# Residual adds and sums of squares of two token quarters moved from VectorE to GpSimd, with the residual's steps two ticks apart, in a hybrid decoder layer

## The chip, the cores and the metric

The kernel is one program on one core of a Trainium2 chip. The metric is the device time of one execution in microseconds, as the median of several runs. Engine names in the profile: PE is TensorE (PEld its weight loads), DVE is VectorE, ACT is ScalarE, POOL is GpSimd, SP is SyncE, which here issues all DMAs of the stage in question.

## The reference, cut to what matters

One decoder layer over 2048 tokens of width 1024, all in f32. Two groups of token mixers (gated DeltaNet and HGRN2, four heads each) give `mix`. Then, with `rms_norm(x, w) = x * rsqrt(mean(x * x) + eps) * w` over the width:

```python
mix_out = jnp.einsum('btc,cd->btd', mix, w_out[i])
h = h + rms_norm(mix_out, post_mix_norm[i])
u = jnp.einsum('btd,df->btf', rms_norm(h, pre_mlp_norm[i]), w_mlp_up[i])
y = jnp.einsum('btf,fd->btd', jnp.square(jax.nn.relu(u)), w_mlp_down[i])
h = h + rms_norm(y, post_mlp_norm[i])
e = rms_norm(jnp.einsum('bte,ed->btd', p[i], w_ple_proj[i]), ple_norm[i])
gate = jax.nn.sigmoid(jnp.einsum('btd,de->bte', h, w_ple_gate[i]))
h = h + e * gate
```

The change lies in the first three of these lines: the output projection, the residual with its norm, and the norm ahead of the up projection.

## The kernel before, in words

**Layout.** The width stands on the 128 partitions, so a matrix of 1024 by 512 tokens is eight tiles of 128x512. The tokens are four quarters `q` of 512. Every f32 matmul operand is split in two fp32r halves, a high one (a ScalarE copy, line 159 or 212) and a low one (a VectorE subtraction, line 160 or 213), and each product of two such operands is three matmuls.

**The output projection** (lines 1283 to 1327) runs over 32 tiles `j`, that is `(q, d)`: four quarters times eight output tiles of 128 columns. A tile is 24 matmuls (`product`, line 1092). `ready_out(j + 2)` and `stage_out(j + 3)` prepare weights ahead: for the first three quarters the raw weights `raw_out` are loaded and split (1024 columns wide, one ScalarE and one VectorE instruction); for the last quarter both halves are reloaded from a copy in DRAM, without a split. After each tile ScalarE copies the PSUM bank to `yo` (line 1319) and squares it; `squares` (line 215) adds the square to `acc_o`. The squares use one buffer, tag `sq`, `bufs=1`, which the norms also use.

**Ticks.** `mm` (line 1085) calls `tick()` ahead of every eighth matmul. `later(gen, offsets)` enters a generator in an agenda; each tick runs one step of what is due. An output tile is three ticks. This sets the order in which instructions are written down; each engine then runs its own queue in that order as a scheduler arranged it, with TensorE's order fixed by hand.

**Norm and residual of the first two quarters.** When a quarter's eight tiles are done, `normed` (line 1169) is entered with the offsets `OUT_STEPS`:

- the first two steps are `rstd_steps` (line 1115): split `acc` to `hl`; then a ones-matmul of two (lines 1121 and 1122) sums over partitions, and ScalarE (Ln, Exp, Square) with VectorE (lines 1125 to 1131) makes `r`, the reciprocal root;
- eight steps of `residual` (line 1148): store the tile before to `h1d`, load the next tile of `x` (tag `late`, two buffers), then `y = y * gain * r` (line 1159), `y = y + x` (line 1160), and through `squares` the square of `y` summed into `acc_h` (line 223);
- one step stores the last tile and splits `acc_h`, and one step is again the norm, which gives `rn`, kept in `h1_r[q]`.

The third and fourth quarters only store `yo` and the norm's row; their residual comes later, inside the up projection (`passed`, line 1180).

**Preparing the up projection.** The up projection is a Strassen product with seven combinations of weight blocks and of columns. `early_operands` (line 1211), entered at tile (2, 1), reloads the first quarter from `h1d`, scales it by `rn` (line 1218) and splits it. Once `h1_r[1]` is there, `up_operands` (line 1222), called `prep`, does the same for the second quarter (line 1237), forms differences (lines 1241, 1242, 1247, 1252) and splits them, one step a tick. The weight blocks come from `u_raw`: blocks "11" and "12" are split at the last tile but one, "22" at the last, with the sums of lines 1303 and 1304; blocks "1", "2" and "4" follow after the last tile (lines 1328 to 1332). The first group of the up projection then multiplies "11" and "12", and after that the other five blocks together, column by column.

**Order on the queues.** SP issues in its own order and waits in place: a store to `h1d` waits for the residual add of its tile, and later loads stand behind it.

Of the kernel before, what the change touches and what calls it, by code (L numbers as in the profile page):

```python
# [15 lines left out]
ALU = mybir.AluOpType  # L16
# [7 lines left out]
KD = D // P  # L24
QT = 512
NQ = T // QT
# [11 lines left out]
R_PREMIX, R_POSTMIX, R_PREMLP, R_POSTMLP, R_PLE = 0, 8, 16, 24, 32  # L38
# [5 lines left out]
N_CONST = C_MASK + len(LEVELS)  # L44


OUT_STEPS = (1, 5) + tuple(range(7, 15)) + (15, 25)
MLP_STEPS = (1, 5) + tuple(range(7, 25, 2))


# [33 lines left out]
def trunk(ctx, tc, x, xT, pT, vecs, w_in, w_ab, gdn_a_log, gdn_dt_bias, w_out, w_up, w_down,  # L84
          w_ple, w_gate, consts, out):
    nc = tc.nc
    V, S, G, PE = nc.vector, nc.scalar, nc.gpsimd, nc.tensor
# [13 lines left out]
    def bank(name, pool=None):  # L101
        return (pool or pm).tile([P, QT], F32, tag="ps", name=name)

    def blk(c):
        return slice(c * P, (c + 1) * P)
# [14 lines left out]
    def col(r):  # L120
        return cols[:, r : r + 1]
# [35 lines left out]
    def split(t, eng, raw):  # L157

        S.activation(t[:, 0], raw, AF.Copy)  # L159
        eng.tensor_tensor(t[:, 1], raw, t[:, 0], ALU.subtract)  # L160
# [54 lines left out]
    def squares(acc, src, k, name, eng=V):  # L215

        if acc is None:
            acc = st.tile([P, QT], F32, tag="acc", name=f"acc_{name}", bufs=3)
            S.activation(acc, src, AF.Square)
        else:  # L220
            sq = st.tile([P, QT], F32, tag="sq", name=f"sq_{name}_{k}", bufs=1)
            S.activation(sq, src, AF.Square)  # L222
            eng.tensor_tensor(acc, acc, sq, ALU.add)  # L223
        return acc
# [7 lines left out]
    def spread_load(rd, name, pool=None, tag="rsb", bufs=2):  # L232
        rsb = (pool or st).tile([P, QT], F32, tag=tag, name=f"rsb_{name}", bufs=bufs)
        nc.sync.dma_start(rsb, rd.broadcast_to([P, QT]))
        return rsb
# [8 lines left out]
    def tok(q):  # L244
        return slice(q * QT, (q + 1) * QT)

    mixd = [[dr.tile([P, QT], F32, name=f"mixd{q}_{k}") for k in range(KD)] for q in range(NQ)]
    h1d = [[dr.tile([P, QT], F32, name=f"h1d{q}_{k}") for k in range(KD)] for q in range(NQ)]
# [99 lines left out]
    with ExitStack() as ectx:  # L348
        es = ectx.enter_context(tc.tile_pool(name="es", bufs=1))
        with tc.manual_schedule(engines={mybir.EngineType.SP}):  # L350
# [34 lines left out]
            rsb = spread_load(x_r[0], "x0")  # L385
# [10 lines left out]
    with mixers as mctx:  # L396
# [605 lines left out]
        with tc.manual_schedule(engines={mybir.EngineType.SP}):  # L1002
# [5 lines left out]
            for j, (name, key, src, q, h, then, g, b) in enumerate(works):  # L1008
# [3 lines left out]
                ps = bank(f"mm_{name}")  # L1012
# [40 lines left out]
            while clock[0] <= last or len(held) < 2 or 1 in ready:  # L1053
                if fill:
                    q, d = fill.pop(0)
# [25 lines left out]
    def later(gen, offsets):  # L1081
        for o in offsets:
            agenda.setdefault(clock[0] + o, []).append(gen)
# [24 lines left out]
    def late(src, name):  # L1108
        t = st.tile([P, QT], F32, tag="late", name=name)
        nc.sync.dma_start(t, src)  # L1110
        return t
# [3 lines left out]
    def rstd_steps(acc, scale, eps, name, done, pool=None, home=None, wait=False):  # L1115

        hl = st.tile([P, 2, QT], F32R, tag="hl", name=f"hl_{name}", bufs=1)
        split(hl, V, acc)
        yield
        ps = bank(f"nrm_{name}", pool or pp)  # L1120
        PE.matmul(ps, ones, hl[:, 0, :], start=True, stop=False)
        PE.matmul(ps, ones, hl[:, 1, :], start=False, stop=True)
        r = home() if home else st.tile([P, QT], F32, tag="rsb", name=f"r_{name}", bufs=2)
        t = st.tile([P, QT], F32, tag="sq", name=f"rr_{name}", bufs=1)
        V.tensor_scalar(acc, ps, scale, eps, ALU.mult, ALU.add)
        S.activation(r, acc, AF.Ln)
        S.activation(r, r, AF.Exp, scale=-0.5)
        S.activation(t, r, AF.Square)
        V.tensor_tensor(t, t, acc, ALU.mult)
        V.tensor_scalar(t, t, -0.5, 1.5, ALU.mult, ALU.add)  # L1130
        V.tensor_tensor(r, r, t, ALU.mult)
        if wait:
            yield
        done(r)
# [10 lines left out]

    kept_rows = []

    def residual(q, y_of, rsb, skip, gain, dst, name, sums=None):

        xk = late(skip(0), f"x{name}{q}_0")  # L1150
        y = y_of(0)
        total, put = None, None
        for d in range(KD):
            yield
            if put:
                nc.sync.dma_start(*put)
            if d + 1 < KD:
                nxt, ynxt = late(skip(d + 1), f"x{name}{q}_{d + 1}"), y_of(d + 1)
            V.scalar_tensor_tensor(y, y, col(gain + d), rsb, ALU.mult, ALU.mult)
            V.tensor_tensor(y, y, xk, ALU.add)  # L1160
            put = dst[d], y
            if sums is not None:
                total = squares(total, y, d, f"{sums}{q}")
            xk, y = nxt, ynxt
        yield
        nc.sync.dma_start(*put)
        return total

    def normed(q, ys, acc, skip, gain, dst, name, sums=None, pool=None):

        rd = []
        yield from rstd_steps(acc, 1.0 / D, EPS, f"{name}{q}", rd.append, pool)
        total = yield from residual(q, lambda d: ys[d], rd[0], skip, gain, dst, name, sums)
        if sums is not None:
            yield from rstd_steps(total, 1.0 / D, EPS, f"{sums}{q}", partial(h1_r.__setitem__, q), pool,
                                  lambda: tp.tile([P, QT], F32, tag="rsn", name=f"rn{q}"))
# [17 lines left out]
    def run(gen):  # L1194
        for _ in gen:
            pass
# [73 lines left out]
    def u_block(n, t, raw):  # L1270
        x[n] = t
        split(t.rearrange("p h k n -> p h (k n)"), V, raw)

    def two_blocks(*them):

        w = wp.tile([P, 2, KD, P], F32R, tag="whl", name=f"w_u{them[0][0]}")
        halves = [w[:, :, : KD // 2], w[:, :, KD // 2 :]]
        for t, it in zip(halves, them):
            if it:
                u_block(it[0], t, it[1])  # L1280
        return halves[1]

    for j, (q, d) in enumerate(order):
        if d == 0:
            ys, acc = [], None
            if q < 2:
                later(mix_operands(q + 1), range(2, 18, 2))
            if q == 1:
                later(mix_operands(3), range(17, 25))
        ready_out(j + 2)  # L1290
        stage_out(j + 3)
        if j == len(order) - 5:
            u_raw = [wp.tile([P, 2, QT], F32, tag="raw", name=f"u_raw{i}", bufs=2) for i in range(2)]
            a1, a2 = w_up[0], w_up[FF // P // 2]
            for t, i, src in ((u_raw[0], 0, a1[:, : KD // 2]), (u_raw[1], 1, a1[:, KD // 2 :]),
                              (u_raw[0], 1, a2[:, : KD // 2]), (u_raw[1], 0, a2[:, KD // 2 :])):
                nc.sync.dma_start(t[:, i].rearrange("p (k n) -> p k n", n=P), src)
        if j == len(order) - 2:
            two_blocks(("11", u_raw[0][:, 0]), ("12", u_raw[1][:, 1]))
        if j == len(order) - 1:  # L1300
            (a11, a21), (s1, s4) = ((t[:, 0], t[:, 1]) for t in u_raw)
            b22 = two_blocks(("22", s1), None)
            V.tensor_tensor(s1, s1, a21, ALU.add)
            V.tensor_tensor(a21, a11, a21, ALU.subtract)
            u_block("3", b22, a21)
        if (q, d) == (2, 1):
            early = early_operands()
            later(early, range(KD))
        if prep is None and h1_r[1] is not None:
            run(early)  # L1310
            prep = up_operands(0, h1_r)
            later(prep, range(0, 24, 1))
        if j in held:
            ps = held.pop(j)
        else:
            ps = bank(f"mmo_{q}_{d}", pp)
            product(ps, columns(ready.pop(j)), xin[q])
        y = ytile(f"yo{q}_{d}") if q < 2 else tp.tile([P, QT], F32, tag="stg", name=f"yo{q}_{d}")
        S.activation(y, ps, AF.Copy)
        acc = squares(acc, ps, d, f"o{q}")  # L1320
        ys.append(y)
        if q >= 2:
            nc.sync.dma_start(yod[q][d], y)
        if d == KD - 1 and q < 2:
            later(normed(q, ys, acc, lambda d, q=q: xT[blk(d), tok(q)], R_POSTMIX, h1d[q], "o", "h"), OUT_STEPS)
        elif d == KD - 1:
            later(rstd_steps(acc, 1.0 / D, EPS, f"o{q}", row_of(o_r, q), po, wait=True), OUT_STEPS[:2] + (9,))
    b2 = two_blocks(("1", s1), None)
    V.tensor_tensor(a11, s1, a11, ALU.subtract)
    u_block("2", b2, a11)  # L1330
    V.tensor_tensor(s4, s4, a11, ALU.subtract)
    u_block("4", wp.tile([P, 2, KD // 2, P], F32R, tag="raw", name="w_u4", bufs=2), s4)
    run(prep)
    octx.close()
# [323 lines left out]
    rsb = {q: spread_load(ple_r[q], f"pg{q}", None, "acc", 3) for q in (0, 1)}  # L1658
    es, puts = {(q, 0): embedded(q, 0, rsb[q]) for q in (0, 1)}, []
    for half in range(2):  # L1660
# [4 lines left out]
        for d in range(KD):  # L1665
# [4 lines left out]
            if d + 1 == KD and half == 0:  # L1670
                rsb = {q: spread_load(ple_r[q], f"pg{q}", None, "acc", 3) for q in (2, 3)}
            for s, q in enumerate(qs):
                ps = bank(f"mmg_{q}_{d}", pp)
# [60 lines left out]
```

## Time and profile before

| what | us |
|---|---|
| median of 3 runs | 2756.56 |
| lowest and highest run | 2754.08, 2765.73 |
| the profiled execution | 2763.47 |
| its span (first to last instruction) | 2761.6 |
| output projection in that trace, first to last matmul | 1136 to 1330 |
| up projection in that trace, first matmul | 1330 |

All times inside the trace are counted from the start of the span. A profile line of an instruction has its start, its duration, the engine, the line of the kernel, the operation, output and inputs by name, shapes and count; in brackets stands the idle time of the engine ahead of it and what ended it. A merged line (x24) has the time from the first start to the last end. Recorded durations of successive instructions on VectorE and ScalarE overlap a little, so what one instruction occupies is read from the next one's start. In a line of waits the numbers are the total in us, how often, and the longest. In a line of one tile's instructions the numbers in the middle are the shortest, median and longest duration in ns, then the first and last start. In the table of stretches PEclk, the granted TensorE clock, is the third number from the end, followed by the DMA share and GB/s.

### The profile page before, as it was taken

The page shows a single profiled execution, that of the slowest core. Times are in us where ns is not written, and L with a number is a line of the kernel's source. Part 1 is how long each engine was busy: PE and PEld are TensorE (multiplying, and loading weights), DVE is VectorE, ACT ScalarE, POOL GpSimd, SP SyncE. Part 2 cuts the span into 40 slices and gives each one's busy share as a digit, 9 for nine tenths or more (in the row PEclk, how much of TensorE's full clock was granted, in tenths as well). Part 3 has the DMA queues.
Part 4 walks back from the last instruction along what each step waited for, and adds up shares of the span by engine and source line. Part 5 has one row for each costly group of instructions (what it writes and reads, how often), then busy time and mean ns, then how long its engine had stood idle before and what let it go on. Part 6 is the DMA issues. An engine that isn't in the chain of part 4 may idle for free.

```text
span 2761.6 us, 38372 instructions
## 1 busy us (share of the span) xinstructions
PE 2672.5 (97%) x12721; PEld 2219.0 (80%) x12721; DVE 2045.6 (74%) x4242; ACT 1469.3 (53%) x2943; POOL 104.4 (4%) x104
## 2 busy tenths in 40 slices
PE   7999999999999999999899999999999999999999
PEld 5788788888888888777788887887888888887887
DVE  6788777787777777577889867857787765567776
ACT  6665555464546445676555645545454545465421
POOL 0000000000000000000000000001000000001000
PEclk9999999999999999999999999999999999999999
DMA  7776776666666665787466547667464456677663
GB/s 262 250 250 224 231 250 234 224 220 226 234 210 217 200 213 174 262 303 246 146 221 221 187 164 245 220 193 241 152 207 147 146 177 203 193 254 236 209 207 133
DMA packets 268598, 589.24 MB, mean 213 GB/s; under 512 B 55642, under 2 KB 59960, under 8 KB 249200
## 3 DMA queue, kind: packets, MB, share of 16 engines
q1 hardware_dynamic: 268400, 586.79, 63.7%
q8 instruction: 101, 1.65, 0.3%
q14 instruction: 97, 0.79, 0.1%
HBM read 419.75 MB, written 166.92 MB: 212 GB/s over the span
## 4 chain that ended last, share of the span: by engine, by line
PE 57%; DVE 9%; DMA 6%; issue 5%; ACT 3%; POOL 1%; SPq 1%; DVEq 0%; POOLq 0%; ACTq 0%
PE u L1090 21%; PE d L1090 20%; PE mmg L1090 6%; PE mm L1020 6%; DVE pr_g L658 1%; DMA ud_g<-u_g 1%; DMA sys_g<-ud_g 1%; PE mmo L1090 1%; DVE xs_g L661 1%; DMA rd_g<-m_g 1%; DMA rsb_g<-rd_g 1%; DMA raw_out<-in_w_out_dram 1%; DVE xs_g L663 1%; DMA db<-hid 1%; DMA mixT<-mixd 0%
## 5 line engine op out<-in xcount | busy, mean ns | idle before, releaser
L1020 PE MATMUL mm<-xt,w 128*128 128x512 f32 x3072 | 771.2, 399 | 3.1 <-ACT qk_h L758 1.5
L1020 PEld LDWEIGHTS mm<-xt,w 128*128 128x128 f32 x3072 | 560.4, 189 | 109.8 <-ACT qk_h L758 1.9
L1090 PE MATMUL d<-db,da 128*128 128x512 f32 x2688 | 617.2, 391 | 6.9 <-ACT db L212 4.9
L1090 PEld LDWEIGHTS d<-db,da 128*128 128x128 f32 x2688 | 507.0, 189 | 116.3 <-ACT db L212 6.7
L1090 PE MATMUL u<-t,wu 128*128 128x512 f32 x2604 | 593.3, 390 | 3.5 <-ACT wu L159 3.4
L1090 PEld LDWEIGHTS u<-t,wu 128*128 128x128 f32 x2604 | 489.6, 188 | 106.4 <-ACT wu L159 4.2
L213 DVE TENSOR_TENSOR db<-db 128x512 fp32r<-128x512 f32 x224 | 160.8, 718 | 76.0 <-ACT db L212 74.8
L1419 DVE TENSOR_TENSOR u<-u,u 128x512 f32<-128x512 f32 x224 | 150.5, 683 | 63.1 <-PE u L1090 61.1
L212 ACT ACTIVATE db<-db 128x512 fp32r<-128x512 f32 x224 | 140.9, 629 | 85.2 <-DMA db<-hid 81.2
L1090 PE MATMUL mmo<-mixT,w_out 128*128 128x512 f32 x720 | 169.2, 395 | 9.6 <-DVE w_out L160 7.1
L1090 PE MATMUL mmg<-h2T,wg 128*128 128x512 f32 x768 | 174.5, 389 | 0.0
L1460 ACT ACTIVATE u<-u 128x512 f32<-128x512 f32 x128 | 80.9, 632 | 168.0 <-DVE u L1419 167.7
L1090 PEld LDWEIGHTS mmo<-mixT,w_out 128*128 128x128 f32 x720 | 137.0, 191 | 40.9 <-DVE w_out L160 8.8
L1090 PEld LDWEIGHTS mmg<-h2T,wg 128*128 128x128 f32 x768 | 144.2, 188 | 29.9
L160 DVE TENSOR_TENSOR da<-da 128x512 fp32r<-128x512 f32 x128 | 94.2, 736 | 88.3 <-ACT da L159 87.9
L159 ACT ACTIVATE da<-da 128x512 fp32r<-128x512 f32 x128 | 80.5, 629 | 136.9 <-DMA da<-sumd 114.7
L159 ACT ACTIVATE wu<-a 128x512 fp32r<-128x512 f32 x124 | 73.9, 622 | 49.2 <-DMA a<-in_w_up_dram 46.6
L658 DVE TENSOR_TENSOR pr_g<-xs_g,sys_g 128x16 f32<-128x16 f32 (+14 forms) x240 | 93.9, 391 | 5.3
L223 POOL TENSOR_TENSOR acc_y<-acc_y,sq_y 128x512 f32<-128x512 f32 x28 | 38.6, 1380 | 1384.1 <-ACT sq_y L222 1383.3
L160 DVE TENSOR_TENSOR wu<-a,wu 128x512 fp32r<-128x512 f32 x124 | 84.9, 688 | 3.9 <-ACT wu L159 3.8
L1461 ACT ACTIVATE u<-u 128x512 f32<-128x512 f32 x128 | 80.7, 631 | 3.7
L160 DVE TENSOR_TENSOR da<-dr,da 128x512 fp32r<-128x512 f32 x96 | 66.3, 691 | 18.2 <-ACT da L159 16.3
(374 smaller groups left out, 3806.9 us busy)
## 6 DMA issues: line engine op xcount, KB each, us to landing
w<-cache_in SPq DMA_DIRECT2D x96, 1024.0 KB
db<-hid SPq DMA_DIRECT2D x224, 256.0 KB
cache_in<-w SPq DMA_DIRECT2D x32, 1024.0 KB
hid<-u SPq DMA_DIRECT2D x128, 256.0 KB
da<-sumd SPq DMA_DIRECT2D x128, 256.0 KB
a<-in_w_up_dram SPq DMA_DIRECT2D x124, 256.0 KB
hid<-ht SPq DMA_DIRECT2D x96, 256.0 KB
dr<-in_w_down_dram SPq DMA_DIRECT2D x96, 256.0 KB
```

The lines of the kernel that those rows point to most:

```text
L159: S.activation(t[:, 0], raw, AF.Copy)
L160: eng.tensor_tensor(t[:, 1], raw, t[:, 0], ALU.subtract)
L212: S.activation(t[:, 0], plain(t), AF.Copy)
L213: V.tensor_tensor(t[:, 1], plain(t), t[:, 0], ALU.subtract)
L223: eng.tensor_tensor(acc, acc, sq, ALU.add)
L658: V.tensor_tensor(pr[:, :, :, 0:i], xs[:, None, :, 0:i].broadcast_to([P, 2, GC, i]), sys[:, 0:i, i : i + 2].rearrange("p j two -> p two j" ...
L661: V.tensor_reduce(xs[:, :, i : i + 2].rearrange("p g two -> p two g"), pr[:, :, :, 0 : i + 1], AX.X, ALU.add)
L1020: PE.matmul(ps, *terms[i], start=i == 0, stop=i == nt - 1)
L1090: PE.matmul(ps, a, b, start=start, stop=stop)
L1419: V.tensor_tensor(c[new], c[old], ps, ALU.add)
L1460: S.activation(c[k], c[k], AF.Relu)
L1461: S.activation(c[k], c[k], AF.Square)
```

## The change

The residual of the first two quarters gets an engine argument: its adds run on GpSimd, and so do its sums of squares but for the last one of each quarter, which stays on VectorE. The sums of squares of the fourth quarter's projection go to GpSimd as well. The offsets in ticks become 3 and 6 for the norm (1 and 5 before), 9, 11, ... 23 for the eight residual tiles (7 to 14 before), 24 and 27 for the last store and second norm (15 and 25 before). The third and fourth quarters' norms, which use the first two offsets, move with them from 1, 5, 9 to 3, 6, 9. `early_operands` takes every second tick from the third on, where it took every tick. Two subtractions of weight blocks are written down ahead of the last tile and no longer behind it.

```diff
-OUT_STEPS = (1, 5) + tuple(range(7, 15)) + (15, 25)
+OUT_STEPS = (3, 6) + tuple(range(9, 25, 2)) + (24, 27)
...
-    def residual(q, y_of, rsb, skip, gain, dst, name, sums=None):
+    def residual(q, y_of, rsb, skip, gain, dst, name, sums=None, eng=V):
...
-            V.tensor_tensor(y, y, xk, ALU.add)
+            eng.tensor_tensor(y, y, xk, ALU.add)
             put = dst[d], y
             if sums is not None:
-                total = squares(total, y, d, f"{sums}{q}")
+                total = squares(total, y, d, f"{sums}{q}", V if d + 1 == KD else eng)
...
-    def normed(q, ys, acc, skip, gain, dst, name, sums=None, pool=None):
+    def normed(q, ys, acc, skip, gain, dst, name, sums=None, pool=None, eng=V):
...
-        total = yield from residual(q, lambda d: ys[d], rd[0], skip, gain, dst, name, sums)
+        total = yield from residual(q, lambda d: ys[d], rd[0], skip, gain, dst, name, sums, eng)
...
             V.tensor_tensor(s1, s1, a21, ALU.add)
             V.tensor_tensor(a21, a11, a21, ALU.subtract)
+            V.tensor_tensor(a11, s1, a11, ALU.subtract)
+            V.tensor_tensor(s4, s4, a11, ALU.subtract)
             u_block("3", b22, a21)
         if (q, d) == (2, 1):
             early = early_operands()
-            later(early, range(KD))
+            later(early, range(3, 3 + 2 * KD, 2))
...
-        acc = squares(acc, ps, d, f"o{q}")
+        acc = squares(acc, ps, d, f"o{q}", G if q == NQ - 1 else V)
...
-            later(normed(q, ys, acc, lambda d, q=q: xT[blk(d), tok(q)], R_POSTMIX, h1d[q], "o", "h"), OUT_STEPS)
+            later(normed(q, ys, acc, lambda d, q=q: xT[blk(d), tok(q)], R_POSTMIX, h1d[q], "o", "h",
+                     eng=G), OUT_STEPS)
...
-    b2 = two_blocks(("1", s1), None)
-    V.tensor_tensor(a11, s1, a11, ALU.subtract)
-    u_block("2", b2, a11)
-    V.tensor_tensor(s4, s4, a11, ALU.subtract)
+    u_block("2", two_blocks(("1", s1), None), a11)
     u_block("4", wp.tile([P, 2, KD // 2, P], F32R, tag="raw", name="w_u4", bufs=2), s4)
```

## Prediction

> **What bounds the kernel now.** I read the page first, for the engines' shares of the whole span, then the waits of the stretch in which the output projection runs (1136 to 1370 us), then TensorE's instructions there in order of time.
>
> ```profile
> PE 2672.5 (97%) x12721; PEld 2219.0 (80%) x12721; DVE 2045.6 (74%) x4242; ACT 1469.3 (53%) x2943; POOL 104.4 (4%) x104
> ```
> ```profile
> ACT w_out L159 <- DMA raw_out<-in_w_out_dram: 13.4, 8, 4.7
> ...
> PE mmo L1090 <- DVE w_out L160: 7.1, 4, 3.1
> ```
> ```profile
> 1230.42 2.11 PE L1090 MATMUL mmo<-mixT,w_out 128*128 128x512 f32 x8 [1.87 <-ACT sq_o L222]
> ...
> 1255.02 5.76 PE L1090 MATMUL mmo<-mixT,w_out 128*128 128x512 f32 x24 [1.16 <-DVE w_out L160]
> 1263.08 7.36 PE L1090 MATMUL mmo<-mixT,w_out 128*128 128x512 f32 x24 [2.30 <-DVE w_out L160]
> 1273.55 14.15 PE L1090 MATMUL mmo<-mixT,w_out 128*128 128x512 f32 x54 [3.11 <-DVE w_out L160]
> ...
> 1295.70 34.62 PE L1090 MATMUL mmo<-mixT,w_out 128*128 128x512 f32 x152
> ...
> 1340.00 6.95 PE L1090 MATMUL u<-t,w_u 128*128 128x512 f32 x16 [4.25 <-ACT w_u L159]
> ```
>
> TensorE is the bound of the kernel as a whole, but not of this stage: there it waits for operands that VectorE and ScalarE split. The gaps from 1228 us on are 1.87 + 1.16 + 2.30 + 3.11 + 4.25 = 12.7 us. Undisturbed, a matmul takes 34.62 / 152 = 0.228 us, so a tick of eight takes 1.82 us and an output tile of 24 takes 5.47. Behind three gaps it is slower: 7.36 us instead of 5.47, 14.15 instead of 12.3, 6.95 instead of 3.64, together 7.1 us. Nothing this change can free in the stage is worth more than 12.7 + 7.1 = 19.8 us.
>
> Who is late is told by a table of stretches. I cut it at the events that gate one another: first residual, its norm, the second projection norm, second residual, its norm, and the preparation of the up projection until the third weight block ("2") is split. (Columns: stretch, its length, then busy us of PE, PEld, DVE, ACT, POOL.)
>
> ```profile
> 1204.00:1232.10 28.10, 26.23 (x116) 21.42 (x115) 25.86 (x40) 18.20 (x32) 0.00 (x0) 1.00 0.89 300
> 1232.10:1246.60 14.50, 14.50 (x65) 11.94 (x65) 11.37 (x17) 11.72 (x16) 0.00 (x0) 1.00 0.77 246
> 1246.60:1256.10 9.50, 8.34 (x38) 6.56 (x37) 7.27 (x12) 7.39 (x12) 0.00 (x0) 1.00 0.16 60
> 1256.10:1286.30 30.20, 24.79 (x94) 19.48 (x93) 26.86 (x41) 14.54 (x25) 0.00 (x0) 0.89 0.79 263
> 1286.30:1295.80 9.50, 9.50 (x44) 7.87 (x43) 5.03 (x9) 7.75 (x12) 0.00 (x0) 1.00 0.96 299
> 1295.80:1341.10 45.30, 41.05 (x179) 33.26 (x177) 41.31 (x68) 27.57 (x47) 0.00 (x0) 0.98 0.66 219
> sum 137.10, PE 124.41 PEld 100.52 DVE 117.71 ACT 87.17 POOL 0.00; mean PE 20.73 PEld 16.75 DVE 19.62 ACT 14.53 POOL 0.00
> ```
> ```profile
> 1203.97 0.75 DVE L1159 SCALAR_TENSOR_TENSOR yo<-yo,cols,r_o 128x512 f32<-128x512 f32 x1
> 1204.63 0.68 DVE L223 TENSOR_TENSOR acc_o<-acc_o,sq_o 128x512 f32<-128x512 f32 x1
> 1205.23 0.69 DVE L1160 TENSOR_TENSOR yo<-yo,xo 128x512 f32<-128x512 f32 x1
> ...
> 1285.65 0.69 DVE L160 TENSOR_TENSOR hl_h<-acc_h,hl_h 128x512 fp32r<-128x512 f32 x1
> ...
> 1340.41 0.68 DVE L160 TENSOR_TENSOR w_u<-u_raw,w_u 128x512 fp32r<-128x512 f32 x1
> ```
>
> The chain is VectorE's: it begins the first residual at 1203.97, comes to the split for the second residual's norm at 1285.65 and to the low half of block "2" at 1340.41, on whose high half TensorE resumed at 1340.00. It is busy 117.7 of those 137.1 us. In the three long stretches it idles only 2.24 + 3.34 + 3.99 = 9.6 us. Successive starts (1203.97, 1204.63, 1205.23) show that an add holds VectorE for 0.60 us and a scaled product for 0.66.
>
> **What moving an add costs.** The stage before has no GpSimd work, so the price comes from the down projection, where GpSimd already adds squares of the same 128x512 f32 shape.
>
> ```profile
> L223 POOL TENSOR_TENSOR acc_y<-acc_y,sq_y x28: 1286/1300/1674, 1741.2 to 2587.2; 128x512 f32<-128x512 f32 x28
> ```
> ```profile
> 1743.24 1.55 POOL L223 TENSOR_TENSOR acc_y<-acc_y,sq_y 128x512 f32<-128x512 f32 x1 [0.74 <-ACT sq_y L222]
> 1745.54 1.62 POOL L223 TENSOR_TENSOR acc_y<-acc_y,sq_y 128x512 f32<-128x512 f32 x1 [0.74 <-ACT sq_y L222]
> ...
> 1923.08 1.30 POOL L223 TENSOR_TENSOR acc_y<-acc_y,sq_y 128x512 f32<-128x512 f32 x1 [0.75 <-ACT sq_y L222]
> ```
> ```profile
> 1742.97 0.68 DVE L213 TENSOR_TENSOR db<-db 128x512 fp32r<-128x512 f32 x1
> 1743.72 1.63 DVE L160 TENSOR_TENSOR da<-da 128x512 fp32r<-128x512 f32 x1
> 1745.27 0.74 DVE L1237 SCALAR_TENSOR_TENSOR b<-b,cols,rsb_n 128x512 f32<-128x512 f32 x1
> 1746.02 1.69 DVE L213 TENSOR_TENSOR db<-db 128x512 fp32r<-128x512 f32 x1
> 1747.63 2.07 DVE L1237 SCALAR_TENSOR_TENSOR b<-b,cols,rsb_n 128x512 f32<-128x512 f32 x3
> ...
> 1923.41 2.47 DVE L1523 TENSOR_TENSOR yu<-yu,d 128x512 f32<-128x512 f32 x4
> ```
>
> This is the row that decides. A split met by a GpSimd add takes 1.63 or 1.69 us instead of 0.69, and the add takes 1.55 or 1.62 instead of 1.30: they take turns. The cost to VectorE: free at 1742.97 + 0.60 = 1743.57, it starts its next but one at 1745.27, so 1.70 for one split of 0.60: **1.10 us lost**. Again from 1745.27 + 0.66 = 1745.93 to 1747.63: 1.70, 1.10 lost. Line 1523, which reads one operand from PSUM, isn't slowed under the add at 1923.08 (2.47 for four). Nearly all VectorE work in our stage reads two operands from SBUF (splits, scaled products, adds); only the norms' lines 1125 and 1130 do not.
>
> The Trainium skill ("SBUF — State Buffer", section "SBUF: two separate sides") says that the pair of ports is held exclusively for the whole instruction and the loser blocks fully. The turns agree; the length differs, 1.10 us in these rows against the recorded 1.30. By the whole instruction the sum below becomes that of rival C.
>
> **The change part by part.**
>
> - *35 adds go to GpSimd*: per quarter eight residual adds and six sums, plus seven sums of the last quarter's squares. VectorE saves 35 x 0.60 = 21.0 us and is held off for 35 x 1.10 = 38.5: **+17.5**. Ends: no add meets it (-21.0), each blocks 1.30 (+24.5). I take 1.10, read under VectorE as dense as here.
> - *Adds that fall where VectorE idles anyway* cost nothing; the idle time of the three stretches is 9.6 us. I take about two thirds: **-6**; ends 0 and -9.6.
> - *Norm steps at ticks 3 and 6 instead of 1 and 5*: the first residual's factor comes one tick later, **+1.8** (ends 0 and 1.8). For the third and fourth quarters the rows are stored and read much later: nothing.
> - *End of the preparation*: in the built program seven VectorE instructions that stood ahead of the split of "2" (last operand columns, fourth norm's split) now follow: 7 x 0.60 = **-4.2**. They are due at the fourth column, 45 matmuls or 10.3 us later; VectorE needs eight instructions, 4.8 us, for them. The two subtractions placed earlier are the same two: 0. If that cover is gone, the 4.2 comes back.
> - *Two ticks a tile, last step 27*: the preparation begins one tile (5.47 us) later on TensorE's clock. Hidden, as VectorE's queue reaches it later still; its last loads stand in SP's queue behind the store of the 31st of 32 tiles, three TensorE tiles (16.4 us) ahead of "2". Uncovered: up to 5.5.
> - *Early operands at 3, 5, ... instead of 0, 1, ...*: eight loads, products and splits, the same, due at the first up product, hidden. Their loads and the weight loads share SP's queue with the residual's stores, which now wait for GpSimd; behind those stand the next x loads (two buffers) and raw weights. An add ends 0.6 to 1 us later than before, but steps are 3.6 us apart instead of 1.8: nothing, or the 13.4 us of waits on raw weights shown above grows or shrinks by a few.
> - *New waits of ScalarE on GpSimd*: squares share one buffer, so a square waits for the sum that reads the one before; behind it in ScalarE's queue stand weight splits and PSUM copies. The row nearest is GpSimd's own wait for a square, 0.74. While GpSimd runs, an idle VectorE loses nothing, so I take 0; the upper end is rival B.
>
> Sum: 17.5 - 6 + 1.8 - 4.2 = **+9.1 us**, all before the resumption now at 1340.00; the work after it is unchanged. The profiled execution took 2763.47 us (span 2761.6), so 2772.6 for it; it lay 6.9 above the median of 2756.56, and from the median the forecast is **2765.7, say 2766**.
>
> **Rivals.**
>
> - *A, faster.* GpSimd's adds fit into VectorE's pauses, VectorE loses 21 us of work, spread over twice the ticks, and the weights come in time. All 19.8 us of gaps and slow matmuls go: 2737. For it: the four gaps named are VectorE's and ScalarE's lateness. Against it: only 9.6 us of pauses for 38.5 us of holding. It decides if under 10 of the 35 adds meet VectorE.
> - *B, slower.* VectorE and GpSimd both stand while ScalarE, in order, makes the square either waits for. 12 squares of the residual and 10 of the projection now stand in line for the one buffer; at 0.75 each that is 16.5, giving +25.6: 2782. For it: every GpSimd add in the rows above shows 0.74 idle ahead of it. Against: VectorE has a queue of splits to fill it. It decides when VectorE's idle time in the two residual stretches exceeds that of before by over 6 us.
> - *C, slower.* Each add holds VectorE for its full 1.30 us: 7.0 more, +16.1: 2773. For: the recorded duration. Against: the 1.10 worked out twice.
>
> **How the numbers follow.** A measurement of this kernel tells about 0.5%, 13.8 us, from no change. Forecast 0.50, A 0.13, B 0.25, C 0.12. The forecast's own range is 2758 to 2771 (idle time filled between 0 and 9.6, cover of the late start partly gone). Faster by over 0.5% (under 2742.8) holds most of A: 0.11. Slower (over 2770.3) holds B but for its weak cases (0.23), most of C (0.08) and the forecast's upper edge (0.03): 0.34. The rest, 0.55, is within. The range goes up to B's value, 2782, and down to 2750, leaving out the full A and the stronger cases of B.
>
> **What would show it.** Right: GpSimd rows L1160 and L223 between 1205 and 1345 us with means of 1.4 to 1.6; VectorE splits and products there of 1.3 to 1.8 us; the second residual's norm split later than 1285.65, near 1295; TensorE resuming on "2" near 1349. Wrong: VectorE rows there still at 0.69 (A); VectorE idle over 25 us in these stretches (B); or a wait on raw weights or PSUM banks that I cost at nothing leading the list of TensorE's waits.

## The result, and the profile after

| | median us | lowest to highest | runs |
|---|---|---|---|
| before | 2757.88 | 2754.08 to 2765.73 | 11 |
| after | 2767.18 | 2761.24 to 2771.20 | 11 |

The ratio is 1.0031 [1.0022, 1.0040], which is +8.6 us (6.1 to 11.0): a small loss, inside the 0.5% that the prediction counted as no change, though these eleven runs of each tell it from zero. The forecast was +9.1, or 2766.

First the engines' line of the page of after.

```profile
PE 2672.6 (97%) x12721; PEld 2218.4 (80%) x12721; DVE 2056.4 (74%) x4207; ACT 1471.4 (53%) x2943; POOL 161.7 (6%) x139
```

VectorE has 35 instructions fewer (4242 before) and is recorded busy 10.8 us longer (2045.6 before). Where that comes from, the start of the first residual shows: GpSimd's instructions in order of time, then VectorE's.

```profile
1205.00 1.52 POOL L1160 TENSOR_TENSOR yo<-yo,xo 128x512 f32<-128x512 f32 x1 [41.47 <-ACT mixT L212]
1207.29 1.54 POOL L1160 TENSOR_TENSOR yo<-yo,xo 128x512 f32<-128x512 f32 x1 [0.77 <-ACT acc_h L219]
1209.57 1.57 POOL L223 TENSOR_TENSOR acc_h<-acc_h,sq_h 128x512 f32<-128x512 f32 x1 [0.74 <-ACT sq_h L222]
...
1294.90 1.27 POOL L223 TENSOR_TENSOR acc_h<-acc_h,sq_h 128x512 f32<-128x512 f32 x1
...
1318.72 1.33 POOL L223 TENSOR_TENSOR acc_o<-acc_o,sq_o 128x512 f32<-128x512 f32 x1 [9.56 <-ACT sq_o L222]
```
```profile
1204.02 0.75 DVE L1159 SCALAR_TENSOR_TENSOR yo<-yo,cols,r_o 128x512 f32<-128x512 f32 x1
1204.69 0.69 DVE L223 TENSOR_TENSOR acc_o<-acc_o,sq_o 128x512 f32<-128x512 f32 x1
1205.29 1.78 DVE L1159 SCALAR_TENSOR_TENSOR yo<-yo,cols,r_o 128x512 f32<-128x512 f32 x1
1206.99 0.68 DVE L213 TENSOR_TENSOR mixT<-mixT 128x512 fp32r<-128x512 f32 x1
1207.60 1.78 DVE L1159 SCALAR_TENSOR_TENSOR yo<-yo,cols,r_o 128x512 f32<-128x512 f32 x1
...
1296.87 0.69 DVE L223 TENSOR_TENSOR acc_h<-acc_h,sq_h 128x512 f32<-128x512 f32 x1 [3.07 <-ACT sq_h L222]
1298.26 0.69 DVE L160 TENSOR_TENSOR hl_h<-acc_h,hl_h 128x512 fp32r<-128x512 f32 x1 [0.70 <-ACT hl_h L159]
...
1320.60 2.45 DVE L1237 SCALAR_TENSOR_TENSOR b<-b,cols,rn 128x512 f32<-128x512 f32 x2 [1.71 <-DMA b<-h1d]
...
1349.04 0.68 DVE L160 TENSOR_TENSOR w_u<-u_raw,w_u 128x512 fp32r<-128x512 f32 x1
```

Read them side by side. The add at 1205.00 lies over the product at 1205.29, which takes 1.78 us instead of 0.75; the add at 1207.29 lies over that at 1207.60, again 1.78. The split between them, at 1206.99, meets no add and takes 0.68. At 1294.90 and 1318.72 VectorE is idle (3.07 and 1.71 us, for a square and for a load), the add runs alone in 1.27 or 1.33, and no row of VectorE is lengthened. The 3.07 us aren't unrelated to GpSimd, though: ScalarE makes the square that VectorE waits for at 1296.21, once the sum of 1294.90 is over.

The groups of VectorE from the first residual (1204 us) to the split of "2" (1349.7) give the sum over the whole stage: first of after, then the like group of before for the one form whose duration isn't shown yet.

```profile
L1159 DVE SCALAR_TENSOR_TENSOR yo<-yo,cols,r_o 128x512 f32<-128x512 f32 x16 | 24.3, 1519 | 0.0
L160 DVE TENSOR_TENSOR w_out<-raw_out,w_out 128x1024 fp32r<-128x1024 f32 x11 | 16.7, 1514 | 2.2 <-ACT w_out L159 2.2
L213 DVE TENSOR_TENSOR mixT<-mixT 128x512 fp32r<-128x512 f32 x11 | 12.6, 1156 | 0.3 <-ACT mixT L212 0.2
...
L223 DVE TENSOR_TENSOR acc_o<-acc_o,sq_o 128x512 f32<-128x512 f32 x13 | 10.9, 837 | 0.7 <-ACT sq_o L222 0.5
...
L1237 DVE SCALAR_TENSOR_TENSOR b<-b,cols,rn 128x512 f32<-128x512 f32 x8 | 9.2, 1168 | 2.9 <-DMA b<-h1d 2.8
...
L160 DVE TENSOR_TENSOR t<-be,t 128x512 fp32r<-128x512 f32 x8 | 7.5, 952 | 1.0 <-ACT t L159 1.0
L1218 DVE SCALAR_TENSOR_TENSOR be<-be,cols,rn 128x512 f32<-128x512 f32 x8 | 7.0, 870 | 0.0
...
L1252 DVE TENSOR_TENSOR b<-be,b 128x512 f32<-128x512 f32 x3 | 4.3, 1420 | 0.0
```
```profile
L160 DVE TENSOR_TENSOR w_out<-raw_out,w_out 128x1024 fp32r<-128x1024 f32 x11 | 13.4, 1219 | 0.3 <-ACT w_out L159 0.3
```

Against 0.75 us for a scaled product, 0.69 for the other 512-wide forms and 1.22 for the wide split, the excess is 12.3 + 3.3 + 5.0 + 1.9 + 3.2 + 2.0 + 1.0 + 2.2 = 30.9 us. At 1.03 to 1.09 for each row held, that is about 29 of the 35 adds; the other six or so met a VectorE that was waiting.

The table of stretches of after, cut at the same events as that of before (its columns are the same):

```profile
1204.00:1240.90 36.90, 30.73 (x125) 23.80 (x123) 34.64 (x31) 19.21 (x32) 23.75 (x14) 0.95 0.64 204
1240.90:1252.70 11.80, 11.50 (x42) 9.03 (x43) 6.21 (x9) 8.65 (x12) 0.00 (x0) 0.86 0.95 344
1252.70:1262.80 10.10, 10.10 (x47) 8.35 (x46) 7.85 (x13) 9.02 (x13) 0.00 (x0) 1.00 0.20 64
1262.80:1298.90 36.10, 29.43 (x111) 22.53 (x109) 32.22 (x29) 15.89 (x28) 23.27 (x14) 0.91 0.69 233
1298.90:1307.10 8.20, 8.09 (x36) 6.70 (x37) 3.79 (x7) 6.75 (x10) 0.00 (x0) 1.00 0.90 318
1307.10:1349.70 42.60, 37.58 (x163) 30.05 (x161) 38.23 (x54) 24.58 (x42) 10.13 (x7) 0.97 0.63 223
sum 145.70, PE 127.43 PEld 100.45 DVE 122.93 ACT 84.10 POOL 57.15; mean PE 21.24 PEld 16.74 DVE 20.49 ACT 14.02 POOL 9.52
```

The six stretches last 145.7 us against 137.1, +8.6. The two residual stretches grew by 8.8 and 5.9 us, with 9 and 12 VectorE instructions fewer in them; the last one, of the preparation, shrank by 2.7. In the three long stretches VectorE idles 2.26 + 3.88 + 4.37 = 10.5 us, as before (9.6). TensorE, in order of time, first of after, then where before has its last gap in common with after:

```profile
1148.38 11.95 PE L1090 MATMUL mmo<-mixT,w_out 128*128 128x512 f32 x52
...
1240.17 0.50 PE L1121 MATMUL nrm_h<-hl_h,ones 128*128 128x512 f32 x1 [2.17 <-ACT hl_h L159]
...
1346.52 0.93 PE L1090 MATMUL u<-t,w_u 128*128 128x512 f32 x2 [2.77 <-ACT w_u L159]
1349.77 7.11 PE L1090 MATMUL u<-t,w_u 128*128 128x512 f32 x22 [2.33 <-DVE w_u L160]
...
1375.32 4.90 PE L1090 MATMUL u<-t,wu 128*128 128x512 f32 x19 [2.56 <-ACT wu L159]
```
```profile
1150.00 10.36 PE L1090 MATMUL mmo<-mixT,w_out 128*128 128x512 f32 x45
...
1366.86 13.36 PE L1090 MATMUL u<-t,wu 128*128 128x512 f32 x51 [2.56 <-ACT wu L159]
```

This execution of after came to the stage 1.6 us earlier (1148.38 against 1150.00; nothing ahead of it is changed) and left it 8.5 us later (1375.32 against 1366.86): the stage is 226.9 us long instead of 216.9, +10.1. I use this length for every kernel below, since the parts outside the stage vary from one execution to the next (the stage begins anywhere between 1140 and 1157 us in the table below).

### The profile page after: what moved, and what is told of

Its sections match the earlier page's. It is cut to its first block, busy times and chain, and to the rows that moved or that the text cites. A ratio compares the mean times of both kernels' runs of the same rounds, so it can differ in the third digit from the quotient of the medians.

```text
span 2764.4 us, 38395 instructions
## 1 busy us (share of the span) xinstructions
PE 2672.6 (97%) x12721; PEld 2218.4 (80%) x12721; DVE 2056.4 (74%) x4207; ACT 1471.4 (53%) x2943; POOL 161.7 (6%) x139
## 4 chain that ended last, share of the span: by engine, by line
PE 63%; DVE 14%; DMA 11%; issue 5%; ACT 4%; SPq 1%; POOL 1%; DVEq 0%; ACTq 0%; POOLq 0%
PE u L1090 21%; PE d L1090 18%; PE mm L1020 12%; PE mmg L1090 6%; DMA ud_g<-u_g 2%; DVE pr_g L658 2%; DMA sys_g<-ud_g 1%; DVE xs_g L661 1%; DMA da<-sumd 1%; DVE xs_g L663 1%; DMA rsb_g<-rd_g 1%; DMA rd_g<-m_g 1%; PE mmo L1090 1%; DMA raw_out<-in_w_out_dram 1%; SPq L638 1%
## 5 line engine op out<-in xcount | busy, mean ns | idle before, releaser
L663 DVE SCALAR_TENSOR_TENSOR xs_g<-xs_g,sys_g 128x4 f32<-128x4 f32 x256 | 58.1, 227 | 28.6 <-DMA sys_g<-ud_g 23.5
```

The costliest lines, as they stand in the source:

```text
L663: V.scalar_tensor_tensor(xs[:, :, i + 1], xs[:, :, i], sys[:, i, i + 1 : i + 2], xs[:, :, i + 1], ALU.mult, ALU.add)
```

## The experiments

**Theory ("turns")**: the loss is that each GpSimd add holds VectorE for more time than it saves; the new places cost nothing. **Rivals**: "places" (the later norm and the later preparation cost it), "ScalarE" (rival B: waits for the one square buffer), and in the background "free" (an add on GpSimd holds nobody). Every kernel was timed in turn with before, whose own median lay between 2751.87 and 2761.24 us from one group of runs to the next; so the ratio is what counts, and the last column is the ratio times 2757.88. The stage is from one profiled execution of each, so a difference of 2 or 3 us in it carries no weight by itself.

| kernel | stage from, to | stage against before | ratio | us |
|---|---|---|---|---|
| after | 1148.38, 1375.32 | +10.1 | 1.0031 [1.0022, 1.0040] | +8.6 |
| places only | 1146.26, 1363.83 | +0.7 | 0.9995 [0.9984, 1.0006] | -1.4 |
| engines only | 1150.90, 1383.56 | +15.8 | 1.0053 [1.0037, 1.0069] | +14.6 |
| 32 extra adds | 1150.85, 1388.88 | +21.2 | 1.0071 [1.0054, 1.0087] | +19.6 |
| 16 extra adds | 1152.17, 1377.21 | +8.2 | 1.0027 [1.0016, 1.0038] | +7.5 |
| 32 extra memsets | 1151.48, 1370.91 | +2.6 | 1.0005 [0.9994, 1.0016] | +1.4 |
| own square buffer | 1157.35, 1384.42 | +10.2 | 1.0032 [1.0020, 1.0043] | +8.8 |
| cached weights | 1151.76, 1368.78 | +0.2 | 0.9981 [0.9972, 0.9990] | -5.2 |
| places, cached | 1151.15, 1367.47 | -0.5 | 0.9988 [0.9976, 0.9999] | -3.3 |
| places, earlier norm | 1150.02, 1363.28 | -3.6 | 0.9981 [0.9971, 0.9991] | -5.2 |
| the same, cached | 1153.89, 1366.19 | -4.6 | 0.9972 [0.9961, 0.9983] | -7.7 |
| earlier norm, last sums | 1150.49, 1362.90 | -4.5 | 0.9968 [0.9956, 0.9979] | -8.8 |
| all three | 1140.23, 1354.20 | -2.9 | 0.9984 [0.9973, 0.9994] | -4.4 |

### Places alone and engines alone

Places only: after, with all 35 adds back on VectorE.

```diff
-        acc = squares(acc, ps, d, f"o{q}", G if q == NQ - 1 else V)
+        acc = squares(acc, ps, d, f"o{q}", V)
...
-                     eng=G), OUT_STEPS)
+                     eng=V), OUT_STEPS)
```

> The changed kernel with all its new places (ticks, order of subtractions) and every add back on VectorE. Theory of turns (an add on GpSimd that reads SBUF holds VectorE off for 1.1 us): 35 adds bring back 21.0 us of VectorE work and take away 38.5 us of holding, so about 11.5 us faster than the changed kernel and 2 us faster than before (-6 to +2), TensorE resuming on block 2 at about 1338 us. Rival 'places' (the later preparation costs the time): still 9 us slower than before. Rival 'ScalarE' (in-order waits on GpSimd's sums): as the theory of turns, not told apart here.

Engines only: before, with the 35 adds on GpSimd and all offsets and places as they were.

```diff
-            later(normed(..., "o", "h"), OUT_STEPS)
+            later(normed(..., "o", "h", eng=G), OUT_STEPS)
...
-        acc = squares(acc, ps, d, f"o{q}")
+        acc = squares(acc, ps, d, f"o{q}", G if q == NQ - 1 else V)
```

> The kernel before with its old places, and the same 35 adds on GpSimd. Theory of turns: 17.5 us more holding less 6 us of idle time, 11.5 us slower than before (6 to 17). Rival 'places': no change. Rival 'ScalarE': the squares stand closer together at one tick a tile, over 20 us slower, with VectorE idle over 15 us in the two residual stretches.

Measured -1.4 (-4.4 to +1.7) and +14.6 (10.2 to 19.0). The loss is the engines', and "places" falls. The wider places may even take something off it: between these engines at the old places and at the new ones lie 14.6 - 8.6 = 6.0 us (the intervals overlap by 0.8; the stages differ by 5.7), where the places by themselves give 1.4. Two things in "engines only" bear on this, TensorE's gaps and a wait of VectorE:

```profile
1227.25 8.30 PE L1090 MATMUL mmo<-mixT,w_out 128*128 128x512 f32 x24 [3.42 <-ACT sq_o L222]
1237.93 2.11 PE L1090 MATMUL mmo<-mixT,w_out 128*128 128x512 f32 x8 [2.39 <-ACT sq_o L222]
...
1284.59 13.57 PE L1090 MATMUL mmo<-mixT,w_out 128*128 128x512 f32 x46 [6.59 <-DVE w_out L160]
...
1357.13 5.35 PE L1090 MATMUL u<-t,w_u 128*128 128x512 f32 x11 [5.32 <-ACT w_u L159]
```
```profile
DVE acc_h L223 <- ACT sq_h L222: 9.6, 2, 5.3
```

With steps a tick (1.82 us) apart and two GpSimd adds to a step, ScalarE comes late to the square that frees the PSUM bank, and TensorE waits for it, 3.42 and 2.39 us here, 6.8 us in three waits over the stage (the third is 0.97). Before has one such wait, the 1.87 shown, and after has none. VectorE waits 9.6 us for the squares of the residual (3.6 before, 4.9 after), and in the two residual stretches it idles 12.6 us, 7.0 more than before: the sign of rival B, though less than the 15 expected here. So at the old places the 14.6 aren't shown to be turns alone. Nor does TensorE's wait by itself tell the two apart, since the kernel with 32 extra adds below, in which no square waits for GpSimd, has 11.1 us of it.

### The price of one add

To before, one or two GpSimd adds are added behind each of the 16 residual adds. They read the finished tile and write a spare one that is not read: they take no work off VectorE and nobody waits for them. The third kernel has two GpSimd memsets of the used `x` tile there instead, which write and don't read.

```diff
             V.tensor_tensor(y, y, xk, ALU.add)
+            if name == "o":
...
+                for _ in range(2):
+                    G.tensor_tensor(spare[0], y, y, ALU.add)
```

The left-out lines make the spare tile. With 16 adds the range is 1; with memsets the last line is `G.memset(xk, 0.0)`.

> The kernel before with nothing moved, and behind each of the 16 residual adds two more adds on GpSimd, 128x512 f32, reading the finished tile and writing a spare tile that nobody reads; no engine waits for them in the stage. Theory of turns: 32 x 1.10 = 35 us of holding, less the idle time they fill, 18 to 35 us slower, with VectorE rows of 1.3 to 1.8 us. Rivals 'places' and 'ScalarE': no change, since no place moves and ScalarE waits for none of them.

> The kernel before with one extra add on GpSimd behind each of the 16 residual adds, where the earlier run had two. 32 of them cost 20 us. Theory of turns: 16 x 1.10 = 17.6 us of holding, of which VectorE's idle time takes up to half; 7 to 13 us slower, about half of the cost of two. If instead the queue of GpSimd, which runs late with two, was what cost the time: under 4 us.

> As the run with extra adds, but the two extra GpSimd instructions write only: two memsets of the used x tile, 128x512 f32, which read nothing. Theory of turns in the form that only a GpSimd instruction that reads SBUF takes VectorE's port: no change (-1 to +3 us), VectorE rows at 0.69 us under a memset. If any GpSimd instruction took the turn: 32 times its length (0.31 us for 128x256 in the trace of before, so an estimate of 0.6): up to 13 us slower.

Measured +19.6 for 32, +7.5 for 16 (0.61 and 0.47 us an add), and +1.4 (-1.7 to +4.4) for 32 memsets. "Free" falls. GpSimd's instructions and VectorE's in order of time in the kernel with 32 adds, then the groups of the kernel with memsets over its two residuals (1205 to 1300 us):

```profile
1206.88 10.36 POOL L1167 TENSOR_TENSOR spare<-yo 128x512 f32<-128x512 f32 x6 [41.25 <-DVE yo L1162]
```
```profile
1211.92 1.52 DVE L1162 TENSOR_TENSOR yo<-yo,xo 128x512 f32<-128x512 f32 x1
1213.37 1.52 DVE L223 TENSOR_TENSOR acc_h<-acc_h,sq_h 128x512 f32<-128x512 f32 x1
```
```profile
L1163 POOL MEMSET xo<- 128x512 f32 x32 | 16.8, 526 | 104.5 <-DVE yo L1160 103.6
...
L160 DVE TENSOR_TENSOR w_out<-raw_out,w_out 128x1024 fp32r<-128x1024 f32 x11 | 13.4, 1217 | 2.2 <-ACT w_out L159 2.2
L1159 DVE SCALAR_TENSOR_TENSOR yo<-yo,cols,r_o 128x512 f32<-128x512 f32 x16 | 11.6, 743 | 0.0
```

Beside the adds VectorE's rows are 1.52 where they were 0.69, so a row loses 0.83 us here and not 1.10, and both times lie at the lower end of what the turns expected. Beside 16.8 us of memsets the wide splits keep their mean of 1.22 and the scaled products theirs of 0.74. So what holds VectorE is a GpSimd instruction that reads. The Trainium skill ("SBUF — State Buffer", section "SBUF: two separate sides") says so: a VectorE instruction with two SBUF inputs contends only with a GpSimd instruction that reads SBUF. The memset's rows agree.

### ScalarE and the one square buffer

After, with the residual's squares in a buffer of their own, so that no residual square waits for a projection's sum or the other way round. It is still one buffer, so a residual square waits for the sum of the one before.

```diff
...
-            sq = st.tile([P, QT], F32, tag="sq", name=f"sq_{name}_{k}", bufs=1)
+            if name in ("h0", "h1"):
+                if not own:
+                    own.append(tp.tile([P, QT], F32, tag="rsn", name="sq_own"))
+                sq = own[0]
+            else:
+                sq = st.tile([P, QT], F32, tag="sq", name=f"sq_{name}_{k}", bufs=1)
```

> The changed kernel, with a buffer of its own for the squares of the two residuals, so that the squares of the projection no longer wait for GpSimd's sums (nor GpSimd's sums for theirs). Theory of turns: the number of adds on GpSimd is the same, so as the changed kernel, 9 us slower than before (6 to 12). Rival 'ScalarE': the waits for the one buffer go, and with them at least half of the loss, under 5 us slower than before.

Measured +8.8, as after (+8.6). ScalarE's leading waits, first of after, then of this kernel:

```profile
ACT sq_h L222 <- DVE acc_o L223: 13.3, 8, 4.0
ACT sq_o L222 <- POOL acc_h L223: 7.5, 8, 1.6
```
```profile
ACT sq_own L229 <- POOL yo L1167: 26.5, 12, 3.9
```

The waits of one kind of square for the other kind's sum are gone, 20.8 us of them, and ScalarE now waits for the add itself. It was early, not late: that is slack, and the shared buffer falls as the cause of the loss at these places. The residual squares' own waits for GpSimd's sums stay (7.3 us in two waits, 5.5 in three in after), so this run doesn't test them.

### What is left to gain in this stage

These kernels keep the residual on VectorE. "Cached" reloads the third quarter's weight halves from the copy in DRAM too, instead of splitting them; "earlier norm" has the wide spacing, but the norm at ticks 1 and 5 and the tiles from 7; "last sums" puts the last quarter's seven sums of squares on GpSimd.

```diff
-    staged_out, ready, RAW = {}, {}, 3
+    staged_out, ready, RAW = {}, {}, 2
```
```diff
-OUT_STEPS = (3, 6) + tuple(range(9, 25, 2)) + (24, 27)
+OUT_STEPS = (1, 5) + tuple(range(7, 23, 2)) + (22, 27)
```

Cached on before, and on places only:

> The kernel before, with the third quarter's output weights reloaded in two halves from the copy in DRAM (as the fourth quarter's are) and not split again: eight splits of 1.13 us less on VectorE and of 1.0 on ScalarE, eight loads of 1 MB in place of 0.5 MB. If VectorE's work sets the time of the stage: 5 to 9 us faster than before. If TensorE or the loads set it: no change, or slower by what the longer loads cost.

> The new places with all adds on VectorE, and the third quarter's weights reloaded without a split. If VectorE's work sets the time: the gains add, 6 to 11 us faster than before. If not: as the places alone, within 2 us of before.

Measured -5.2, at the edge of what was expected, and -3.3, which misses: the gains don't add. Nor does the profiled execution of "cached" show a shorter stage (+0.2): VectorE's splits are gone, but TensorE now waits at 1275.20 for the reload. Where the 5.2 us come from stays open.

```profile
1275.20 14.66 PE L1090 MATMUL mmo<-mixT,w_out 128*128 128x512 f32 x56 [6.45 <-DMA w_out<-cache_out]
```

The next two are places only with the earlier norm, and the same cached:

> All adds on VectorE, early operands two ticks apart and subtractions early as in the changed kernel, but the offsets (1, 5), 7, 9, ... 21, 22, 27: the residual two ticks earlier than in the changed kernel and the norm's matmuls in the same place. In the run with the places only TensorE stands 3.46 and 4.35 us at the two norms' matmuls for the split of the sums. If the placing of the norm is what is left to gain there: 4 to 8 us faster than before. If VectorE's sum of work sets the time whatever the place: within 3 us of before.

> The earlier residual and the third quarter's weights reloaded without a split, all adds on VectorE. Each alone was about 5 us faster than before. If both take work or lateness from VectorE's chain: they add in part, 6 to 10 us faster. If TensorE or the loads have become the limit: 3 to 6 us faster, as each alone.

Measured -5.2 and -7.7, both as expected. "Places only" had TensorE wait for the residual's norm, and the earlier norm leaves less of it:

```profile
PE nrm_h L1121 <- ACT hl_h L159: 7.8, 2, 4.3
```

With the earlier norm the two waits are 2.75 and 2.10 us, 4.9 together: 2.9 us less, of 3.8 gained (the intervals overlap; the stages differ by 4.3). Last, the seven sums on GpSimd, on the earlier norm and on the cached one:

> The earlier residual with all residual adds on VectorE, and only the seven sums of the last quarter on GpSimd. Theory of turns: 7 x (1.10 - 0.60) = 3.5 us of VectorE's time, less what falls in its pauses: 0 to 4 us slower than the earlier residual alone (which was 5 us faster than before), so 1 to 5 us faster than before. If an add on GpSimd were free for VectorE: 4 us faster still, 9 us faster than before.

> Before with the wider places of the run with the earlier norm (first norm at ticks 1 and 5, residual tiles every second tick from 7), two raw weight tiles, and the last quarter's seven sums of squares on GpSimd; all residual adds on VectorE. The places and the two raw tiles alone gave -7.7 us; the places and the seven sums alone -8.8, against -5.2 for the places. If the seven sums take turns with VectorE at 1.10 for 0.60 they cost 7 x 0.50 = 3.5 us at most: -4 to -8. If they fall into VectorE's pauses, as the second of those runs leaves open, they save up to 7 x 0.60 = 4.2 us: -9 to -12. A result of -8 to -9 leaves the matter of the seven sums open.

Measured -8.8 and -4.4. The first missed what the turns expected (-1 to -5) and met what was expected if the seven adds were free (-9); the second falls in the range of the turns. Moving the seven sums changed the time by -3.6 in one pair and +3.3 in the other, and the stage by -0.9 and +1.7: no effect that these runs can tell, and I leave open whether it is a small gain or loss. Their rows, GpSimd's and VectorE's in "earlier norm, last sums", show both sides of it:

```profile
1307.29 1.67 POOL L223 TENSOR_TENSOR acc_o<-acc_o,sq_o 128x512 f32<-128x512 f32 x1 [1.24 <-ACT sq_o L222]
...
1324.98 1.31 POOL L223 TENSOR_TENSOR acc_o<-acc_o,sq_o 128x512 f32<-128x512 f32 x1 [6.38 <-ACT sq_o L222]
```
```profile
1309.12 1.44 DVE L1237 SCALAR_TENSOR_TENSOR b<-b,cols,rn 128x512 f32<-128x512 f32 x2 [1.31 <-DMA b<-h1d]
...
1325.05 1.79 DVE L1252 TENSOR_TENSOR b<-be,b 128x512 f32<-128x512 f32 x1
```

The add at 1307.29 falls for the most part into a wait for a load (1.31 idle, up to 1309.12); that at 1324.98 holds a difference up for 1.1 us. Of the kernels run, the four with the earlier norm are 4 to 9 us faster than before, and so faster than after by more; their intervals overlap, so none is shown to be the best.

## Why the prediction was right, step by step

- **The price of an add, right.** Predicted 1.10 us of holding for 0.60 saved. Rows held by an add are 1.78 instead of 0.69 to 0.75. Rival C's 1.30 isn't seen.
- **The main term, right in size.** Predicted 38.5 of holding less 6 for adds that fall where VectorE idles: 32.5. The rows give 30.9. I had taken two thirds of 9.6 us of idle time; about six adds met a waiting VectorE, 6 x 1.06 = 6.4. VectorE's idle time didn't shrink with it (10.5 us against 9.6); the residual's last sums now wait for GpSimd and ScalarE (the 3.07 at 1296.87).
- **First norm a tick later, right.** From the start of the stage to the first residual: 1204.02 - 1148.38 = 55.64 us against 1203.97 - 1150.00 = 53.97, +1.67; predicted +1.8.
- **Seven instructions behind the split of "2", right in kind.** From the split for the second residual's norm to that split: 1349.04 - 1298.26 = 50.78 us against 1340.41 - 1285.65 = 54.76, so -4.0, predicted -4.2. That is a net of more than this term: the seven adds of the last quarter lie within (4.2 saved, and about 5.4 lost under the five that met VectorE), and two sums of the third quarter came ahead of the stretch (-1.2); so the close agreement is in part chance. The table counts 44 VectorE instructions fewer in all (143 against 187, an instruction across a cut counting twice): the 35 adds, these seven, one projection sum that came ahead of the first residual, and one at a cut. The -4.2 doesn't come back: the stage is +10.1 longer at 1375.32, and +8.6 + 1.7 = +10.3 had been lost by the split.
- **The sum, and the luck in it.** From the start of the stage to the split of "2" the two profiled executions differ by +10.3. The terms as measured: 30.9 - 21.0 = +9.9 for the adds (forecast 17.5 - 6 = 11.5), +1.7, -4.2, -0.6 for the projection sum that came earlier, and +3.4 of new idle time of VectorE, which the forecast had at nothing. Of that, 0.9 lies in the three long stretches and 2.5 in the stretch of the first norm, where VectorE idles 11.80 - 6.21 = 5.6 us against 14.50 - 11.37 = 3.1, waiting for splits and a square of ScalarE. What made it wait longer there isn't shown. The adds came out 1.6 below the forecast and the idle time 3.4 above it: that +9.1 lies so close to +8.6 is partly luck.
- **Places: right as a sum, open part by part.** The place terms were 1.8 - 4.2 = -2.4 and measured -1.4 (-4.4 to +1.7). "Earlier norm" came out 3.8 us ahead of "places only", with overlapping intervals. If that holds, the late start of the residual costs more than its tick, since TensorE then waits for the second norm, and the spacing gives something back that I had at zero.
- **ScalarE's waits on GpSimd at nothing: right in the residual stretches, not in general.** In these two stretches VectorE idles 2.26 + 3.88 = 6.1 us, against 2.24 + 3.34 = 5.6 before; rival B needed 6 more. At the old places it idles 7.0 more than before, so there B's sign does appear.
- **Rival A, wrong**, as the rows of 1.78 show. At 29 adds met, its limit of 10 is far.
- **Where the text was off:** it put the split for the second norm near 1295, that is +9.3; it came at 1298.26, +12.6 (+14.2 counted from the start of the stage). By the prediction's own terms the -4.2 comes only after this point, so 1295 was a slip in placing, not in the sum. The lower end of the forecast's own range, 2758, doesn't follow from its terms: with all 9.6 us of idle time filled and no late tick they give 17.5 - 9.6 - 4.2 = +3.7, or 2760. TensorE took up the high half of "2" at 1346.52 for two matmuls and the low half at 1349.77, the 1349 named. GpSimd's sums average 1.57 us, within the 1.4 to 1.6 that I gave, but its residual adds 1.73, since they too are held up by VectorE (the group of after):

```profile
L1160 POOL TENSOR_TENSOR yo<-yo,xo 128x512 f32<-128x512 f32 x16 | 27.6, 1728 | 71.7 <-ACT mixT L212 41.5 <-DVE yo L1159 28.1 <-DMA xo<-in_xT_dram 1.4
```

## What to carry to other kernels

Before an elementwise instruction with SBUF operands is moved from VectorE to GpSimd, look up a row of VectorE that lies under a GpSimd instruction of the same shape, and compare what it loses with what the move saves (here 1.10 against 0.60). Here VectorE was busy nine tenths of the three long stretches, and the move lost. Count as free only the adds that fall into VectorE's own waits, and check that these waits aren't for the moved work itself. Wider places for a side chain and another engine for it are two changes: try them apart, since here one paid (with the norm left early) and the other did not.

## What the runs showed of the hardware that I had not expected

- An add on GpSimd that reads one tile twice and writes another holds VectorE for less than one that reads two tiles and writes back into one of them: rows of 1.52 us (0.83 lost) in the kernel with 32 extra adds, against 1.78 (1.03 to 1.09 lost) in after. The add itself is shorter by about as much: its shortest row is 1.04 us, against 1.27 in after. Which of the two differences makes it shorter, no run here tells.

```profile
L1167 POOL TENSOR_TENSOR spare<-yo x32: 1039/1368/3127, 1206.9 to 1307.1; 128x512 f32<-128x512 f32 x32
```

- A GpSimd memset of 128x512 f32 took 0.53 us, and 32 of them among VectorE's two-operand instructions left these at their usual durations.
